# Layer B's residual read and added in the background, and sums of squares placed later on TensorE

## The chip, the cores and the metric

The kernel runs on one core of one Trainium2 chip. The metric is the time of one execution in microseconds of the device, a median over runs. A core has five engines that run side by side, each through its own queue, in program order: TensorE (PE in the profile) multiplies matrices, VectorE (DVE) and GpSimd (POOL) do elementwise work, ScalarE (ACT) does copies and functions, and SyncE (SP) issues the DMA transfers between the chip's memory (DRAM) and the on-chip memories. Matmul results arrive in PSUM, eight banks of 128 x 512 fp32, and everything else lies in SBUF.

## The reference

The reference is a decoder with two layers on 512 tokens and 16 learned meta tokens, width 2048. Layer A is a gated linear recurrence, layer B an attention with a forget gate. In its last part, which the change touches most, it computes

```python
h = h + fox_mix(h, ...)      # layer B: 16 heads, then  return (o * jax.nn.silu(z)) @ w_out
return h[:, N_META:]         # the meta tokens are dropped
```

Here `o * silu(z)` is a 512 x 2048 matrix, `w_out` is 2048 x 2048, and `h` is the residual, the output of layer A. Inside both layers vectors are normalised by `rms_norm(x, g) = x * rsqrt(mean(x*x) + eps) * g`, in layer B each head's q. The `mean(x*x)` are the sums of squares of the title.

## The kernel before, in words

**Precision.** Every fp32 matrix is split into a high part (a copy to the fp32r type on ACT) and a low part (the difference, on DVE), and a product of two matrices is three matmuls: high by high, high by low, low by high. For weights these are the tiles `w_raw` (as read), `w_hi` and `w_lo`; for the gated attention output they are `sh` and `sl`.

**The output projection of layer B** (lines 1861 to 1987) runs over four column blocks of 512 output columns, n = 0 to 3. Each block uses four PSUM tiles `pts`, one per 128 tokens, and adds products over 16 row groups k of 128 rows. Block 0 is plain: for each k four `o_step`s of three matmuls of 512 columns, 192 in all. Blocks 1 to 3 (`wide`, line 1887) save multiplications with a Strassen-like scheme over eight of the row groups: first four plain k as a lead (48 matmuls of 512 columns), then products 1, 6, 7, 5 into PSUM tiles `pp` of their own, then products 2, 4, 3 added into `pts` (7 x 24 matmuls of 256 columns), then the last four plain k (48 of 512 columns). Products 6, 7, 5, 3 use sums of row halves (`so`, formed once by `pair_sums` on POOL, `sums_o`), and products 6, 7, 5, 4 use sums of weight blocks (`w_sum`, made on DVE). Products 1, 6, 7, 5 make up the blocks `v1`, `v6`, `v7`, which POOL adds into the residual tile `hres`. The last step of a block is `ot = pts + hres` on DVE for each of four token groups, and a transfer of `ot` to DRAM. The two PSUM pools `psj` and `psj2` of four banks swap after each block, so that `pp` of a block takes over the banks of `pts` of the block before.

**The residual** lies in DRAM in a blocked form, `h1y`. `residual(n)` (line 1864) reads it by 16 transfers into `hraw` (one buffer) and rearranges it by four ACT copies into `hres` (two buffers). Block 0 does this after its last matmul in the program, a wide block at its very beginning, before its lead.

**Weights.** `Weights` (from line 218) keeps a list of units in the order of use. Raw weights are read through eight `w_raw` buffers, up to seven reads ahead of the unit in use (`dma_ahead=7`); a buffer is free again when the last unit that uses it has been split. Units are split up to a few ahead. `W.step()` (line 429) does as much of this as fits.

**What sets the order.** The whole program is written out by one Python program that keeps a planner's clock of every engine (`Clock`, line 39), and the order in which it emits instructions is the order in each engine's queue, SP's too. After every few matmuls `tick()` (line 719) calls `W.step()` and then goes once through the list `bg` of background tasks, which are generators. `do(f, ...)` (line 630) holds a task back until the planner's clock says that the instruction could start at most 900 ns (`LEAD`) after the time that PE has reached; a matmul in the background is held back until its inputs are written 1000 ns (`MARGIN`) before PE would come to it. `spin()` (line 727) advances the planner's PE clock by 150 ns without a matmul and calls `tick()`. So the planner decides on an order; on the chip each engine waits only for its own operands.

**Sums of squares.** Per token they are summed by a transpose and a reduction on DVE into `part`, and then by a small matmul of `part` with the constant `group` on PE (`token_sums`, line 664, for layer A, K and the stream; in `att_q`, line 1672, for the q of layer B, eight matmuls of 4 columns). The wait loops ahead of them, lines 670 and 1693, use the 1000 ns margin. In `att_q` the result leads to the factor `ry` (`qy` in the profile) that scales the scores `s` into logits `lg`.

Of the kernel before, what the change touches and what calls it, by code (L numbers as in the profile page):

```python
# [7 lines left out]
F32 = mybir.dt.float32  # L8
F32R = mybir.dt.float32r
AF = mybir.ActivationFunctionType  # L10
ALU = mybir.AluOpType
# [3 lines left out]
P = 128  # L15
D = 2048
KT = D // P
NH = 16
NM = 16
S = 512  # L20
# [8 lines left out]
NB3 = 1  # L29
# [458 lines left out]
def trunk(  # L488
# [5 lines left out]
    clock = Clock()  # L494
# [4 lines left out]
    def opened(stack, name, **kw):  # L499
        return Pool(stack.enter_context(tc.tile_pool(name=name, bufs=1, reuse_waits="tile", **kw)), name, clock)  # L500
# [61 lines left out]
    st_r = ExitStack()  # L562
# [16 lines left out]
    group = cp.tile([P, P], F32, name="group")  # L579
# [48 lines left out]
    act = se.activation  # L628

    def do(f, *args, **kw):  # L630

        while not f.fits(args, kw):
            yield
        f(*args, **kw)
# [29 lines left out]
    def token_sums(sq, t, w, psum, drop):  # L664

        nb = -(-w // 32)
        yield from fold(t, sq, w)
        part = cp.tile([P, 17], F32, name="part", tag="part", bufs=2)[:, :nb]
        yield from do(ve.tensor_reduce, part, folded(t[:, :32 * nb]), axis=mybir.AxisListType.X, op=ALU.add)
        while not te.matmul.fits((), {"lhsT": group, "rhs": part}):  # L670
            yield
        pt = yield from psum()
        te.matmul(pt[:, :nb], lhsT=group, rhs=part, start=True, stop=True)
        ss = cp.tile([P, 17], F32, name="ss", tag="ss", bufs=2)[:, :nb]
        yield from do(ve.tensor_copy, ss, pt[:, :nb])
        drop(pt)
        return ss
# [23 lines left out]
    bg = []  # L701
# [11 lines left out]
    def add(out, a, b):  # L713
        ve.tensor_tensor(out, a, b, op=ALU.add)
# [12 lines left out]
    def spin():  # L727

        clock.free["PE"] += 150
        tick()  # L730
# [285 lines left out]
    def blocks_in(t, d, nb):  # L1016

        for c in range(4):
            yield from do(sy.dma_start,
                t[c * 32:(c + 1) * 32],  # L1020
                d.rearrange("(g q) (c x) -> q g c x", q=32, c=4)[:, :, c, :])

    def blocks_now(t, d, nb):
        for c in range(4):
            sy.dma_start(
                t[c * 32:(c + 1) * 32],
                d.rearrange("(g q) (c x) -> q g c x", q=32, c=4)[:, :, c, :])

# [275 lines left out]
    for h in range(NH):  # L1304
        hd = {"h": h}
        if h == 0:
# [7 lines left out]
            raw = []  # L1314
# [111 lines left out]
    for n in range(KT):  # L1426
# [12 lines left out]
        g = h1_steps(n, pt, xr)  # L1439
# [232 lines left out]
    def att_q(h, uq):  # L1672
        a = A[h] = {"fin": set()}
        while sdone[0] < h:
            yield
        bg.append(att_load(h))
        sq = tb.tile([P, S], F32, name="nsq", tag="nsq")
        yield from do(act, sq, uq, AF.Square)
        g = gqs[:, h:h + 1]
        qh = tb.tile([P, 3 * P], F32R, name="qh", tag="qh")  # L1680
        ql = tb.tile([P, 3 * P], F32R, name="ql", tag="ql")
        yield from do(act, qh, uq[:, P:], AF.Identity, scale=g)
        yield from do(ve.scalar_tensor_tensor, ql, uq[:, P:], g, qh.bitcast(F32), ALU.mult, ALU.subtract)
        qg = tb.tile([P, P], F32, name="qg", tag="qg")
        yield from do(ge.tensor_scalar, qg, uq[:, :P], g, None, ALU.mult)
        free_u("buq")
        a.update(qg=qg, q=(qh, ql))
        ss, y, t1, t2 = (tb.tile([P, 4], F32, name=n, tag=n, bufs=2) for n in ("qs", "qy", "qt1", "qt2"))
        t = tb.tile([P, S], F32, name="nss", tag="nss")
        yield from fold(t, sq, S)  # L1690
        part = cp.tile([P, 17], F32, name="part", tag="part", bufs=2)[:, :16]
        yield from do(ve.tensor_reduce, part, folded(t), axis=mybir.AxisListType.X, op=ALU.add)
        while not te.matmul.fits((), {"lhsT": group, "rhs": part}):
            yield
        pt = psj.tile([P, 512], F32, name="pj1", tag="pj", bufs=pjb[0])
        for j in range(4):
            te.matmul(pt[32 * j:32 * (j + 1), :4], lhsT=group[:, :32],
                      rhs=part.rearrange("p (i j) -> p j i", j=4)[:, j], start=True, stop=True)
        yield from do(ve.tensor_copy, ss, pt[:, :4])
        yield from rstd_steps(y, ss, P, t1, t2)  # L1700
        a["ry"] = y
# [159 lines left out]
    movo = LazySplit(S)  # L1861
    outv = out[0].rearrange("(b p) n -> p b n", p=P)

    def residual(n):

        raw = ob.tile([P, 4, S], F32, name="hraw", tag="hraw")
        hr = ob.tile([P, 4, S], F32, name="hres", tag="hres", bufs=2)
        for j in range(4):
            blocks_now(raw[:, j, :].rearrange("p (g x) -> p g x", g=4), h1y[4 * n + j], 4)
        for b in range(4):  # L1870
            act(hr[:, b, :].rearrange("p (j f) -> p j f", f=32),
                raw.rearrange("p j (g b f) -> p (j g) b f", g=4, f=32)[:, :, b, :], AF.Copy)
        return hr

    def finish(n, b, pt, hr):
        ot = ob.tile([P, S], F32, name="ot", tag="ot", bufs=4)
        ve.tensor_tensor(ot, pt, hr[:, b, :], op=ALU.add)
        sy.dma_start(outv[:, b, n * 512:(n + 1) * 512], ot)

    def o_step(pt, w, k, b, first, last):  # L1880
        wh, wl, _ = w
# [5 lines left out]
    def wide(n):  # L1887

        us = nt_unit[("bo", n)]
        comb = residual(n)  # L1890

        def cb(r, c):
            return comb[:, 2 * r:2 * r + 2, c * 256:(c + 1) * 256]

        def x(e, r):
            return lambda i, q: [t[:, (2 * r + q) * P:(2 * r + q + 1) * P] for t in movo[2 * i + e]]
# [16 lines left out]
        def add(out, a, b):  # L1913
            ve.tensor_tensor(out, a, b, op=ALU.add)
# [8 lines left out]
        for v, xs in ((1, x(0, 0)), (6, s(0, 1)), (7, s(1, 0)), (5, s(0, 0))):  # L1923
            while v == 6 and sums_o in bg:
                spin()
            pp[v] = psj2.tile([P, 512], F32, name="pj1", tag="pj", bufs=4)
            product(v, xs, [v4(pp[v])[:, q] for q in range(2)])
            if v != 5:
                vv[v] = ob.tile([P, 512], F32, name=f"v{v}", tag=f"v{v}")
            if v == 1:  # L1930
                act(vv[1], pp[1], AF.Copy)
                ge.tensor_tensor(cb(0, 0), cb(0, 0), v4(vv[1]), op=ALU.add)
            elif v == 6:
                add(vv[6], pp[6], vv[1])
            elif v == 7:
                add(vv[7], pp[7], vv[6])
                ge.tensor_tensor(cb(1, 0), cb(1, 0), v4(vv[7]), op=ALU.add)
            else:
                add(vv[6], pp[5], vv[6])
                add(vv[7], pp[5], vv[7])  # L1940
                ge.tensor_tensor(cb(0, 1), cb(0, 1), v4(vv[6]), op=ALU.add)
                ge.tensor_tensor(cb(1, 1), cb(1, 1), v4(vv[7]), op=ALU.add)
        for v, xs, r, c in ((2, x(1, 0), 0, 0), (4, x(1, 1), 1, 0), (3, s(1, 1), 0, 1)):
            product(v, xs, [pts[2 * r + q][:, c * 256:(c + 1) * 256] for q in range(2)], False)
        tail = 3 if n == ng - 1 else 0
        for k in range(2 * KB + LEAD, KT - tail):
            w = W.get(us["k", k])
            for b in range(4):
                o_step(pts[b], w, k, b, False, k == KT - 1)
        wt = [W.get(us["k", k]) for k in range(KT - tail, KT)]  # L1950
        for b in range(4):
            ot = ob.tile([P, S], F32, name="ot", tag="ot", bufs=4)
            for k, w in enumerate(wt, KT - tail):
                o_step(pts[b], w, k, b, False, k == KT - 1)
            add(ot, pts[b], comb[:, b, :])
            sy.dma_start(outv[:, b, n * 512:(n + 1) * 512], ot)

    ng = D // 512
# [1 line left out]
    for n in range(ng):  # L1960
        if n >= NB3:
            wide(n)
            psj, psj2 = psj2, psj
            continue
        pts = [psj.tile([P, 512], F32, name="pj1", tag="pj", bufs=4) for _ in range(4)]
        units_n = nt_unit[("bo", n)]
        for k in range(KT):
            if n == 0 and k == 10:
                drain()
                pss.close()  # L1970
                st_l.close()
                so = opened(st_l, "b_sums")
                psj2 = opened(pss, "psj_o", space=PSUM)
                sums_o = pair_sums(movo, lambda j: so.tile([P, S], F32R, name=f"so{j}", tag=f"so{j}"),
                                   lambda j: so.tile([P, S], F32, name=f"sm{j}", tag=f"sm{j}"), S_o, KB, S, ge)
                W.more(lambda nm, w, dt: so.tile([P, w], dt, name=nm, tag=nm), 4, len(W.units))
                bg.append(sums_o)
            w = W.get(units_n[k])
            for b in range(4):
                o_step(pts[b], w, k, b, k == 0, k == KT - 1)  # L1980
        if n == 0:
            st_r.close()
            ob = opened(st_r, "b_out", side="right")
            hr = residual(n)
        psj, psj2 = psj2, psj
        for b in range(4):
            finish(n, b, pts[b], hr)
    drain()
    pss.close()
    st_r.close()  # L1990
# [32 lines left out]
```

## Time and profile before

| | |
|---|---|
| median of 3 runs | 2060.08 us (2059.97 to 2061.24) |
| the profiled execution | 2068.14 us, of which the span from first to last instruction is 2066.4 us |
| mean granted TensorE clock | 0.986 of full speed |
| PE, busy | 2004.8 us (97%), 14676 matmuls |
| DVE, busy | 1522.8 us (74%) |
| ACT, busy | 948.0 us (46%) |
| POOL, busy | 445.4 us (22%) |
| issues of weight reads for the last stage | 64 of 256 KB, 3.7 us to landing in the median |

Busy time is the time in which an engine executes instructions; issuing DMAs does not count as such. Almost every line of the profile bears L194, because one helper emits all instructions, so they are told apart by the names of the tiles: `pj` are the PSUM tiles of the projections, and numbers of buffers are left out, so `w_sum` stands for all weight sums and `v` for `v1`, `v6` and `v7`. Times in a timeline count from the first instruction. A number in brackets at the end of a row is the idle time of the engine just ahead of it, and what it waited for.

### The profile page before, as it was taken

How to read it: one execution, taken by the hardware profiler on the slowest of the kernel's cores; microseconds unless marked ns; L12 is line 12 of the kernel's file. 1: busy time of each engine (PE TensorE's matmuls, PEld its weight loads, DVE VectorE, ACT ScalarE, POOL GpSimd, SP SyncE). 2: the span in 40 equal slices, each digit the busy share in tenths (PEclk: the TensorE clock that was granted, in tenths of full speed). 3: DMA queues.
4: the chain of work that ended last, by engine and by line, in shares of the span. 5: the costliest groups of instructions: out<-in, count | busy, mean ns of one | idle time of the engine just before them, and what ended most of it. 6: DMA issues, size and time to landing. Idle time of an engine off the chain costs nothing.

```text
span 2066.4 us, 39517 instructions
## 1 busy us (share of the span) xinstructions
PE 2004.8 (97%) x14676; PEld 1871.9 (91%) x14676; DVE 1522.8 (74%) x3025; ACT 948.0 (46%) x1756; POOL 445.4 (22%) x527
## 2 busy tenths in 40 slices
PE   8999999999999999999999999999999999999798
PEld 7999999999999999899999999998777777877687
DVE  6878888888888886544498777866777777777554
ACT  6655454545454454423333333334555555554322
POOL 2121111111112121111100000002444433455111
PEclk9999999999999999999999999999999999999899
DMA  8333333333334335345534444465555565553342
GB/s 265 99 111 107 107 110 113 107 106 107 106 107 118 107 110 178 90 154 161 162 86 135 125 134 111 117 187 154 154 149 153 159 165 141 148 144 112 123 136 94
DMA packets 454337, 271.21 MB, mean 131 GB/s; under 512 B 77936, under 2 KB 420448, under 8 KB 454128
## 3 DMA queue, kind: packets, MB, share of 16 engines
q1 hardware_dynamic: 452576, 264.16, 44.8%
q0 software_dynamic: 1536, 4.52, 0.6%
q8 instruction: 115, 1.88, 0.4%
q14 instruction: 78, 0.64, 0.1%
q10 hardware_dynamic: 32, 0.01, 0.0%
HBM read 220.30 MB, written 48.28 MB: 130 GB/s over the span
## 4 chain that ended last, share of the span: by engine, by line
PE 77%; DMA 6%; DVE 5%; SPq 4%; issue 3%; ACT 2%; POOL 2%; ACTq 0%; DVEq 0%; POOLq 0%
PE pj L194 71%; SPq L194 4%; DMA py<-pd 3%; PE o L194 2%; PE tr L194 2%; PE pat L194 1%; DVE w_lo L194 1%; POOL sm L194 1%; DVE lg L194 1%; DMA w_raw<-in_b_w_in_dram 1%; POOL D L194 1%; ACT w_hi L194 1%; PE s L194 1%; DVE sm L194 1%; DMA w_raw<-in_b_w_out_dram 1%
## 5 line engine op out<-in xcount | busy, mean ns | idle before, releaser
L194 PE MATMUL pj<-sh,w_hi 128*128 128x264 f32 (+1 forms) x2604 | 755.2, 314 | 4.3 <-ACT sh L194 3.3
L194 PE MATMUL pj<-sl,w_hi 128*128 128x264 f32 (+1 forms) x2604 | 737.6, 307 | 1.1 <-DVE sl L194 1.1
L194 PE MATMUL pj<-sh,w_lo 128*128 128x264 f32 (+1 forms) x2604 | 736.2, 307 | 1.2 <-DVE w_lo L194 1.2
L194 DVE TENSOR_TENSOR w_lo<-w_raw,w_hi 128x512 fp32r<-128x512 f32 (+1 forms) x585 | 431.8, 751 | 86.7 <-ACT w_hi L194 85.7
L194 PEld LDWEIGHTS pj<-sh,w_hi 128*128 128x128 f32 x2604 | 467.6, 190 | 25.6 <-ACT sh L194 3.9
L194 PEld LDWEIGHTS pj<-sh,w_lo 128*128 128x128 f32 x2604 | 466.4, 189 | 24.5 <-DVE w_lo L194 2.2
L194 PEld LDWEIGHTS pj<-sl,w_hi 128*128 128x128 f32 x2604 | 468.3, 190 | 20.0 <-DVE sl L194 1.8
L194 ACT ACTIVATE w_hi<-w_raw 128x512 fp32r<-128x512 f32 (+1 forms) x585 | 353.3, 621 | 176.3 <-PE pj L194 137.3
L194 PE MATMUL pj<-sm,w_hi 128*128 128x264 f32 x896 | 172.9, 289 | 0.0
L194 PEld LDWEIGHTS pj<-sm,w_hi 128*128 128x128 f32 x896 | 138.5, 188 | 1.7
L194 ACT ACTIVATE w_hi<-w_sum 128x512 fp32r<-128x512 f32 x102 | 63.2, 625 | 162.9 <-POOL w_sum L194 88.7
L194 PE MATMUL pj<-sm,w_lo 128*128 128x264 f32 x448 | 127.4, 284 | 0.0
L194 POOL TENSOR_TENSOR w_sum<-w_sum,w_raw 128x512 f32<-128x512 f32 x28 | 43.6, 1556 | 374.4 <-DVE w_sum L194 195.4
L194 ACT ACT_TABLE_LOAD x87 | 111.6, 1283 | 11.6 <-DVE uq L194 3.8
L194 PE MATMUL pj<-kh,w_hi 128*128 128x264 f32 x460 | 115.6, 285 | 0.0
L194 PE MATMUL pj<-kl,w_hi 128*128 128x264 f32 x460 | 115.1, 284 | 0.0
L194 PE MATMUL pj<-kh,w_lo 128*128 128x264 f32 x460 | 114.7, 283 | 0.0
L194 DVE TENSOR_TENSOR w_lo<-w_sum,w_hi 128x512 fp32r<-128x512 f32 x102 | 80.8, 793 | 15.8 <-ACT w_hi L194 15.0
L194 PE MATMUL pj<-w_hi,sh 128*128 128x512 f32 (+1 forms) x232 | 84.0, 362 | 4.8 <-ACT sh L194 4.8
L194 PE MATMUL pj<-kh,sh 128*128 128x264 f32 x324 | 87.2, 285 | 0.0
L194 PE MATMUL pj<-kl,sh 128*128 128x264 f32 x324 | 86.9, 284 | 0.0
L194 PE MATMUL pj<-kh,sl 128*128 128x264 f32 x324 | 86.8, 284 | 0.0
(387 smaller groups left out, 3610.4 us busy)
## 6 DMA issues: line engine op xcount, KB each, us to landing
w_raw<-in_a_w_in_dram SPq DMA_DIRECT2D x256, 256.0 KB, 3.4
w_raw<-in_kv_w_dram SPq DMA_DIRECT2D x128, 256.0 KB, 4.1
w_raw<-in_b_w_in_dram SPq DMA_DIRECT2D x128, 256.0 KB, 3.2
w_raw<-in_a_w_out_dram SPq DMA_DIRECT2D x64, 256.0 KB, 4.0
w_raw<-in_b_w_out_dram SPq DMA_DIRECT2D x64, 256.0 KB, 3.7
xr<-xT SPq DMA_DIRECT2D x16, 264.0 KB, 4.4
h1T<-h SPq DMA_DIRECT2D x16, 264.0 KB, 2.0
kT<-kn SPq DMA_DIRECT2D x16, 264.0 KB, 2.1
```

What stands on the lines that cost most here:

```text
L194: ins = f(*args, **kw)
```

## The change

Five things change.

1. The wait loops ahead of the matmuls of the sums of squares ask for 2000 ns instead of 1000 between the end of the reduction and the matmul.
2. `residual(n)` becomes a background task: its 16 reads and four copies are emitted one by one when they fit. Block 0's is read by the task `finish`, which is put on the list when block 0's matmuls are emitted; the same task goes on to read residual 1. The residuals 2 and 3 are put on the list in the block before, after product 5.
3. `finish` also holds the four adds and transfers of block 0. Before block 1 emits product 1, it spins until `finish` has emitted them.
4. The adds of `v1`, `v6`, `v7` into `hres` become background tasks (`add_block`), which wait until the residual is there. The add of product 5 into `v7` moves into the task of that block, behind the POOL add that reads `v7`. A wide block spins until its tasks are through before it emits its final adds (in the last block: before its last three k).
5. The pool of the output buffers is opened two k earlier, inside block 0.

```diff
-        while not te.matmul.fits((), {"lhsT": group, "rhs": part}):
+        while clock.ready("PE", [], [part], 2 * clock.MARGIN) > clock.free["PE"]:
             yield
 ...
+    hres = {}
+
     def residual(n):
 
         raw = ob.tile([P, 4, S], F32, name="hraw", tag="hraw")
+        for j in range(4):
+            yield from blocks_in(raw[:, j, :].rearrange("p (g x) -> p g x", g=4), h1y[4 * n + j], 4)
         hr = ob.tile([P, 4, S], F32, name="hres", tag="hres", bufs=2)
-        for j in range(4):
-            blocks_now(raw[:, j, :].rearrange("p (g x) -> p g x", g=4), h1y[4 * n + j], 4)
         for b in range(4):
-            act(hr[:, b, :].rearrange("p (j f) -> p j f", f=32),
-                raw.rearrange("p j (g b f) -> p (j g) b f", g=4, f=32)[:, :, b, :], AF.Copy)
-        return hr
-
-    def finish(n, b, pt, hr):
-        ot = ob.tile([P, S], F32, name="ot", tag="ot", bufs=4)
-        ve.tensor_tensor(ot, pt, hr[:, b, :], op=ALU.add)
-        sy.dma_start(outv[:, b, n * 512:(n + 1) * 512], ot)
+            yield from do(act, hr[:, b, :].rearrange("p (j f) -> p j f", f=32),
+                          raw.rearrange("p j (g b f) -> p (j g) b f", g=4, f=32)[:, :, b, :], AF.Copy)
+        hres[n] = hr
+
+    def block_of(n, r, c):
+        return hres[n][:, 2 * r:2 * r + 2, c * 256:(c + 1) * 256]
+
+    adding = []
+
+    def add_block(n, r, c, v, more=None):
+
+        adding.append((n, r, c))
+        if more is not None:
+            while (n, r, 0) in adding:
+                yield
+            yield from do(ve.tensor_tensor, v, more, v, op=ALU.add)
+        while n not in hres:
+            yield
+        t = block_of(n, r, c)
+        yield from do(ge.tensor_tensor, t, t, v.rearrange("p (q n) -> p q n", q=2), op=ALU.add)
+        adding.remove((n, r, c))
+
+    def finish(n, pts):
+
+        adding.append(n)
+        yield from residual(n)
+        for b in range(4):
+            ot = ob.tile([P, S], F32, name="ot", tag="ot", bufs=4)
+            yield from do(ve.tensor_tensor, ot, pts[b], hres[n][:, b, :], op=ALU.add)
+            yield from do(sy.dma_start, outv[:, b, n * 512:(n + 1) * 512], ot)
+        adding.remove(n)
+        yield from residual(n + 1)
 ...
     def wide(n):
-        comb = residual(n)
 ...
         for v, xs in ((1, x(0, 0)), (6, s(0, 1)), (7, s(1, 0)), (5, s(0, 0))):
             while v == 6 and sums_o in bg:
                 spin()
+            while n == NB3 and NB3 - 1 in adding:
+                spin()
 ...
             if v == 1:
                 act(vv[1], pp[1], AF.Copy)
-                ge.tensor_tensor(cb(0, 0), cb(0, 0), v4(vv[1]), op=ALU.add)
+                bg.append(add_block(n, 0, 0, vv[1]))
 ...
             else:
                 add(vv[6], pp[5], vv[6])
-                add(vv[7], pp[5], vv[7])
-                ge.tensor_tensor(cb(0, 1), cb(0, 1), v4(vv[6]), op=ALU.add)
-                ge.tensor_tensor(cb(1, 1), cb(1, 1), v4(vv[7]), op=ALU.add)
+                bg.append(add_block(n, 0, 1, vv[6]))
+                bg.append(add_block(n, 1, 1, vv[7], pp[5]))
+                if n < ng - 1 and n >= NB3:
+                    bg.append(residual(n + 1))
 ...
+        while adding:
+            spin()
         for b in range(4):
 ...
-            add(ot, pts[b], comb[:, b, :])
+            add(ot, pts[b], hres[n][:, b, :])
 ...
+            if n == 0 and k == KT - 2:
+                movo.upto(KT)
+                st_r.close()
+                ob = opened(st_r, "b_out", side="right")
 ...
-        if n == 0:
-            st_r.close()
-            ob = opened(st_r, "b_out", side="right")
-            hr = residual(n)
         psj, psj2 = psj2, psj
-        for b in range(4):
-            finish(n, b, pts[b], hr)
+        bg.append(finish(n, pts))
```

## Rows read from the trace of the kernel before

**Rows 1.** The page, part 1: busy us, share of the span, instructions of each engine.
```profile
PE 2004.8 (97%) x14676; PEld 1871.9 (91%) x14676; DVE 1522.8 (74%) x3025; ACT 948.0 (46%) x1756; POOL 445.4 (22%) x527
```

**Rows 2.** Waits of TensorE, whole span: us in total, times, longest us.
```profile
PE pj L194 <- ACT w_hi L194: 17.1, 4, 12.0
PE pj L194 <- DVE part L194: 9.4, 7, 2.6
...
PE s L194 <- DVE lg L194: 3.1, 2, 2.9
```

**Rows 3.** Timeline of TensorE, blocks 0 and 1: start, us, operation [idle before <-releaser].
```profile
1909.53 0.40 PE L194 MATMUL pj<-w_hi,sh 128*128 128x512 f32 x1
...
1916.25 0.39 PE L194 MATMUL pj<-w_hi,sl 128*128 128x512 f32 x1
1916.48 0.28 PE L194 MATMUL pj<-w_hi,sh 128*128 128x256 f32 x1
...
1919.20 0.28 PE L194 MATMUL pj<-w_hi,sl 128*128 128x256 f32 x1
1931.48 0.58 PE L194 MATMUL pj<-w_hi,so 128*128 128x256 f32 x1 [11.99 <-ACT w_hi L194]
```

**Rows 4.** Timeline of TensorE, blocks 2 and 3.
```profile
1975.90 0.28 PE L194 MATMUL pj<-w_hi,sh 128*128 128x256 f32 x1
...
1980.76 0.38 PE L194 MATMUL pj<-w_hi,so 128*128 128x256 f32 x1 [1.86 <-ACT w_hi L194]
...
2024.20 0.28 PE L194 MATMUL pj<-w_hi,sh 128*128 128x256 f32 x1
...
2029.93 0.58 PE L194 MATMUL pj<-w_hi,so 128*128 128x256 f32 x1 [2.72 <-ACT w_hi L194]
...
2061.39 0.40 PE L194 MATMUL pj<-w_hi,sl 128*128 128x512 f32 x1
```

**Rows 5.** Stretches: length, busy us of the engines, PEclk, DMA share, GB/s.
```profile
1900.00:1910.00 10.00, 9.80 (x42) 8.01 (x43) 9.13 (x8) 2.39 (x5) 9.76 (x9) 1.00 0.00 0
...
1930.00:1940.00 10.00, 7.68 (x31) 6.80 (x32) 8.10 (x13) 4.60 (x8) 0.21 (x1) 0.50 0.25 81
...
1980.00:1990.00 10.00, 8.40 (x43) 7.91 (x44) 8.73 (x13) 5.09 (x9) 1.76 (x1) 0.66 0.27 88
...
2030.00:2040.00 10.00, 9.36 (x55) 8.77 (x56) 9.05 (x14) 4.58 (x9) 1.76 (x1) 0.70 0.29 99
```

**Rows 6.** Timeline of SP's queue, the issue of DMAs, first two seams.
```profile
1890.66 7.58 SPq L194 DMA_DIRECT2D hraw<-h1y  x16
...
1913.29 3.60 SPq L194 DMA_DIRECT2D out_dram<-ot  x4
1917.06 7.54 SPq L194 DMA_DIRECT2D hraw<-h1y  x16
1924.65 2.48 SPq L194 DMA_DIRECT2D w_raw<-in_b_w_out_dram  x5
...
1966.11 8.53 SPq L194 DMA_DIRECT2D hraw<-h1y  x16
1974.73 14.58 SPq L194 DMA_DIRECT2D w_raw<-in_b_w_out_dram  x9
```

**Rows 7.** Timelines of ACT, DVE and POOL at the first two seams.
```profile
1911.84 2.18 ACT L194 ACTIVATE hres<-hraw 128x512 f32<-128x512 f32 x4
...
1911.97 0.69 DVE L194 TENSOR_TENSOR so<-sm,so 128x512 fp32r<-128x512 f32 x1 [0.15 <-ACT so L194]
1912.58 2.48 DVE L194 TENSOR_TENSOR ot<-pj,hres 128x512 f32<-128x512 f32 x4
1928.40 0.69 DVE L194 TENSOR_TENSOR w_sum<-w_raw 128x512 f32<-128x512 f32 x1 [13.35 <-DMA w_raw<-in_b_w_out_dram]
...
1981.27 1.76 POOL L194 TENSOR_TENSOR hres<-hres,v 128x512 f32<-128x512 f32 x1 [32.05 <-ACT v L194]
```

**Rows 8.** DMA issues: operation, count, KB each, median us from issue to landing.
```profile
hraw<-h1y SPq DMA_DIRECT2D x64, 64.0 KB, 2.1
```

More of the change, by code (lines that the diff above doesn't have):

```diff
@@ L1019, in blocks_in @@
             yield from do(sy.dma_start,
[L1020 to L1025, printed above, removed]
                 t[c * 32:(c + 1) * 32],
@@ L1692, in att_q @@
         yield from do(ve.tensor_reduce, part, folded(t), axis=mybir.AxisListType.X, op=ALU.add)
-        while not te.matmul.fits((), {"lhsT": group, "rhs": part}):
+        while clock.ready("PE", [], [part], 2 * clock.MARGIN) > clock.free["PE"]:
             yield
@@ L1889, in wide @@
         us = nt_unit[("bo", n)]
-        comb = residual(n)
-        def cb(r, c):
-            return comb[:, 2 * r:2 * r + 2, c * 256:(c + 1) * 256]
         def x(e, r):
@@ L1936, in wide @@
                 add(vv[7], pp[7], vv[6])
-                ge.tensor_tensor(cb(1, 0), cb(1, 0), v4(vv[7]), op=ALU.add)
+                bg.append(add_block(n, 1, 0, vv[7]))
             else:
                 add(vv[6], pp[5], vv[6])
-                add(vv[7], pp[5], vv[7])
-                ge.tensor_tensor(cb(0, 1), cb(0, 1), v4(vv[6]), op=ALU.add)
-                ge.tensor_tensor(cb(1, 1), cb(1, 1), v4(vv[7]), op=ALU.add)
+                bg.append(add_block(n, 0, 1, vv[6]))
+                bg.append(add_block(n, 1, 1, vv[7], pp[5]))
+                if n < ng - 1 and n >= NB3:
+                    bg.append(residual(n + 1))
         for v, xs, r, c in ((2, x(1, 0), 0, 0), (4, x(1, 1), 1, 0), (3, s(1, 1), 0, 1)):
```

## The prediction

> **What bounds the kernel now.** I read the busy times of the page first, then the waits of TensorE, then the timeline around the longest of them, and last the queues of the engines that TensorE waited for. TensorE is busy 97% of the span [rows 1], so only time in which it stands still, or runs at the lower clock, can be won. Its list of waits is short. One line leads it: 17.1 us in four waits for the high half of a weight (ACT w_hi), the longest 12.0 us; the second is 9.4 us in seven waits for `part`, the partial sums of squares [rows 2]. Every other line is below those.
>
> The four waits on w_hi lie in the last stage, the output projection of layer B, which the change rewrites. To see what that stage loses I price its matmuls where they run undisturbed: 30 matmuls of 512 columns start from 1909.53 to 1916.25, so 6.72/29 = 0.232 us each; the 24 of 256 columns of product 1 start from 1916.48 to 1919.20, so 0.118 us each [rows 3]. A wide block has 96 of the first and 168 of the second: 22.3 + 19.8 = 42.1 us. Product 1 of the three wide blocks starts at 1916.48, 1975.90 and 2024.20 [rows 3, 4]: the first period is 59.4 us, the second 48.3, so 17.3 and 6.2 us too long. From 2024.20 to the last matmul at 2061.39 it is 37.2 us, against 168 x 0.118 + 48 x 0.232 = 31.0: 6.2 too long. **Lost in the stage: 29.7 us.** In each period the loss sits between products 1 and 6: 11.99 us of waiting at 1931.48, 1.86 at 1980.76, 2.72 at 2029.93 [rows 3, 4], and behind each gap a stretch granted 0.50, 0.66 and 0.70 of the full clock [rows 5], so partly or wholly the 1.2 GHz level.
>
> Why is w_hi late? Product 6 needs a sum of two weight blocks (w_sum). Its DVE instruction starts at 1928.40, after standing idle for 13.35 us until a weight had landed [rows 7]. That weight was read late because of SP's queue, which is strictly in program order: it issued the reads of residual 0 from 1890.66, then held four output transfers that waited for the last adds (1913.29), then sixteen reads of residual 1 (7.54 us from 1917.06), and only at 1924.65 the next weight reads. At the next seam the weights start at 1974.73, behind residual reads that hold the queue for 8.53 us [rows 6].
>
> **The change part by part.** Apart from order, nothing is added: per block still 16 residual reads on SP, 4 copies on ACT, 4 adds on POOL (none for block 0), 4 adds on DVE, 4 output transfers.
>
> *Reads of residuals 2 and 3.* They move from the head of a wide block into the second half of the block before it. On SP they leave some 8.5 us per seam [rows 6] to the weight reads, which then follow the four output transfers directly: the reads that started at 1974.73 start near 1966.1. Product 1 ends near 1978.8, and the wait was 1.86 us, so they are early by some 6 us. SP has room: a block issues 16 weight reads, 16 residual reads and 4 outputs, 36 x 0.47 = 17 us of 42. The reads wait for the single raw buffer, which the ACT copies of the residual before have left long ago; were they late, the weight reads would be queued behind them, and TensorE behind those. The four copies on ACT (2.18 us, [rows 7]) move past weight splits that are made several units ahead. These two seams lose 12.4 us; I leave 2 of it, for the adds that now run beside the weight work: gain 10.4, bounds 4 and 12.4.
>
> *Residual 0 and the end of block 0.* Reads, copies, adds and outputs of block 0 become a background task that starts when the block's matmuls are issued, and product 1 of the next block may not be issued before it is through, since it takes over block 0's PSUM buffers. This is a new wait on TensorE: behind it stands everything. The planner gives the task 11.1 us of lead matmuls (48 x 0.232). The 16 reads take 7.5 us to issue, one lands in 2.1 us [rows 8], the copies take 2.2, the first add 0.7: 12.5 us if it started only with the lead. But SP has been idle since 1898, so on the chip the reads go out early, between the weight reads that step in at each k. The first add can start as before, near 1912.6, when the last split of the pair sums (the `so` at 1911.97) is done [rows 7]; product 1 wants its buffer at 1916.48. The wait of 12.0 us goes. What is late next is DVE: from 1912.6 to the start of the fourth product it has 4 adds of block 0, 6 sums, 6 low halves and 2 adds to do, 18 x 0.62 = 11.2 us (0.62 from the four adds in 2.48 us, [rows 7]), in 12.4 us. That packs only if their order is right, so of 17.3 us I leave 4 (a short wait and some slow clock): gain 13.3. Bounds: 0, if the seam stalls as long on its new wait, and 17.3.
>
> A rule speaks against these two parts. The trace shows that sixteen issues hold SP for 7.54 us while one such read lands in 2.1 us [rows 6, 8]. The Trainium skill, "DMA: Bandwidth & Descriptors", section "Issuing engines are not separate DMA queues", says that the time a sequencer needs to initiate a DMA is usually small beside the DMA itself. By that rule the place of the reads in the queue would matter little and the sum would shrink to its last term; by the row it is the place that costs. Small strided reads are where I side with the row.
>
> *Adds of the blocks (POOL) and the last product.* The four adds per wide block are issued once the residual is there. The DVE add of product 5 into v7 waits, as before, until POOL has read v7; low halves are queued behind it. The final adds wait for POOL too. Cost taken 0: POOL does nothing else there, and the last add of a block needs TensorE's last matmul anyway. If POOL were late at the very end, one of its adds, 1.76 us [rows 7], would show: bound 2.
>
> *Sums of squares later on TensorE.* The planner now keeps 2000 instead of 1000 ns between the reduction on DVE and the matmul that uses it, so about four more 512-column matmuls go ahead of it. In layer B seven groups waited, 9.4 us, the longest 2.6 us [rows 2]. Each gets shorter by up to 1 us: at most 7.0; some are shorter than 1 us, so I take 6. Lower bound 0, if TensorE then waits for the logits instead; upper bound 9.4. In the first layer and for K, TensorE shows no wait on `part`: taken 0, bound 3 lost where a later result reaches the end of a stage.
>
> Sum: 10.4 + 13.3 + 6 = 29.7, rounded to 30 us. The profiled execution took 2068.1 us, 8.1 above the median of 2060.1 (its span is 2066.4); 2068.1 - 30 = 2038 under the profiler, and the same off the median is **2030 us**.
>
> **Rivals.** (1) *The first seam stays.* The background task is drawn out by its sixteen waits for the planner's clock, or DVE works off weight sums ahead of block 0's adds, and product 1 stalls where product 6 did. For it: the 12.5 us chain against 11.1 us of lead. Against: the reads may run ahead on SP. Then 17.3 us stay and 10.4 + 6 = 16 go: 2044. (2) *Bytes, not places.* Each residual is 1 MB in small pieces; if weights land late because both share the DMA engines, moving helps nothing, and only the 6 us of `part` are won: 2054. This is the skill's rule above turned into a time. Against: the queue was held, not the engines, and no bytes moved from 1900 to 1910, just before the wait [rows 5]. (3) *Slower.* The later sums of squares delay the factor that scales the logits, so the three PSUM tiles of the scores come free later and TensorE waits for `lg` in every head, as it did once for 2.9 us [rows 2]. At 2.9 us in 16 heads that is 46 us against 30 won: 2076. It decides from 30/16 = 1.9 us per head. Against: the line holds 3.1 us in all, so 14 of the 16 heads have slack on this path. (4) *No net change.* Order in the first layers shifts with the new margin and loses what the end wins: 2060.
>
> **How the numbers follow.** Chances: forecast 0.64, (1) 0.19, (2) 0.05, (3) 0.07, (4) 0.05. Faster by over 0.2% (4.1 us, about what a measurement can tell): 0.64 + 0.19 + 0.05 = 0.88; within: 0.05; slower: 0.07. Range: with all gains at their upper bounds, 12.4 + 17.3 + 9.4 = 39, it is 2021, so the low end is 2020; the high end, 2050, takes in rival (1) with the lower bound of the other seams (4 instead of 10.4: 2048). That leaves out (2), (3) and (4), 0.17, and a little of the tails.
>
> **What would show it.** The waits of TensorE on w_hi near 1931, 1980 and 2030 gone or under 2 us, no stretch below 0.9 of the clock after 1900; w_raw reads directly behind the output transfers on SP; periods of the wide blocks near 43 to 46 us; the line on `part` below 4 us. A wait of product 1 on the adds of block 0 means rival (1); longer waits on `lg` mean rival (3); weights that still land late, though issued early, mean rival (2).

## The result, and the profile after

| | before | after |
|---|---|---|
| median | 2060.66 us (2059.97 to 2066.78, 4 runs) | 2038.34 us (2034.93 to 2041.51, 4 runs) |
| ratio of the two | | 0.9885, 95% interval 0.9869 to 0.9900 |
| the profiled execution | 2068.14 us, span 2066.4 | 2041.51 us, span 2039.8 |
| mean granted TensorE clock | 0.986 | 0.993 |

The change makes the kernel 22.3 us faster by the medians, 23.7 by the ratio (21 to 27 by its interval) and 26.6 us by the two profiled executions. The forecast was 2030 us.

TensorE is again the engine that is nearly always busy; it does the same 14676 matmuls in 7.6 us less [rows 1]. Page, part 1, after:

```profile
PE 1997.2 (98%) x14676; PEld 1863.2 (91%) x14676; DVE 1519.3 (74%) x3025; ACT 950.3 (47%) x1757; POOL 439.5 (22%) x527
```

The waits of TensorE over the whole span after (us in total, times, longest):

```profile
PE o L194 <- ACT PTh L194: 5.7, 6, 2.1
PE pj L194 <- ACT sh L194: 4.6, 4, 1.6
PE s L194 <- DVE lg L194: 4.6, 2, 2.8
...
PE pj L194 <- DVE part L194: 3.2, 4, 1.5
PE pj L194 <- ACT w_hi L194: 2.8, 1, 2.8
```

Against [rows 2], the line on w_hi has gone from 17.1 us in four waits to one of 2.8, and the one on `part` from 9.4 to 3.2. But a line that was lower down before, the matmuls of `o` (a head's output) that wait for `PTh` (the high part of the transposed scores), now leads.

Where in time the gain lies is read from the timeline of TensorE after. A seam is the passage from one column block to the next, and a period runs from one product 1 to the next. The rows show product 1 of the three wide blocks, the one wait left, and the last matmul (start, us, operation, idle before).

```profile
1914.23 0.28 PE L194 MATMUL pj<-w_hi,sh 128*128 128x256 f32 x1
...
1920.70 0.58 PE L194 MATMUL pj<-w_hi,so 128*128 128x256 f32 x1 [2.75 <-ACT w_hi L194]
...
1962.32 0.28 PE L194 MATMUL pj<-w_hi,sh 128*128 128x256 f32 x1
...
2004.46 0.28 PE L194 MATMUL pj<-w_hi,sh 128*128 128x256 f32 x1
...
2035.22 0.40 PE L194 MATMUL pj<-w_hi,sl 128*128 128x512 f32 x1
```

With [rows 3, 4] this splits the 26.17 us by which the last matmul starts earlier (all in us):

| stretch | before | after | gain | forecast |
|---|---|---|---|---|
| up to product 1 of block 1 | 1916.48 | 1914.23 | 2.25 | 6 |
| first period | 59.42 | 48.09 | 11.33 | 13.3 |
| second period | 48.30 | 42.14 | 6.16 | 10.4 for the two |
| from 2024.20 / 2004.46 to the last matmul | 37.19 | 30.76 | 6.43 | |

The second and third period are now as long as their matmuls take undisturbed (42.1 and 31.0); the first still has 6 us too much. The stretches of the clock agree (length, busy us of the engines, PEclk, DMA share, GB/s): the stretch with the wait of 2.75 us is granted 0.66. The two at the later seams, which had 0.66 and 0.70 [rows 5], get the full clock.

```profile
1920.00:1930.00 10.00, 9.15 (x53) 8.86 (x54) 8.99 (x15) 5.65 (x10) 0.00 (x0) 0.66 0.75 221
1965.00:1975.00 10.00, 10.00 (x86) 10.00 (x85) 8.68 (x14) 5.48 (x10) 2.04 (x2) 1.00 0.48 157
...
2010.00:2020.00 10.00, 10.00 (x86) 10.00 (x86) 10.00 (x14) 4.84 (x8) 4.24 (x3) 1.00 0.16 56
```

What is left at the first seam shows in SP's queue after, against [rows 6] (issue of DMAs: start, us, transfer, count):

```profile
1889.37 7.58 SPq L194 DMA_DIRECT2D hraw<-h1y  x16
1897.05 0.39 SPq L194 DMA_DIRECT2D w_raw<-in_b_w_out_dram  x1
1912.87 1.82 SPq L194 DMA_DIRECT2D out_dram<-ot  x2
1914.78 0.39 SPq L194 DMA_DIRECT2D w_raw<-in_b_w_out_dram  x1
1915.27 0.92 SPq L194 DMA_DIRECT2D out_dram<-ot  x2
...
1951.32 2.13 SPq L194 DMA_DIRECT2D out_dram<-ot  x4
1953.54 21.62 SPq L194 DMA_DIRECT2D w_raw<-in_b_w_out_dram  x12
```

The reads of residual 0 still go out early and in one piece. At 1897.05 one weight read follows, and then SP stands for 15 us in front of two output transfers of block 0; the next weight read leaves only at 1914.78. At the second seam the weights follow the outputs directly, as forecast. Why the outputs were late, and what hung on the read behind them, ACT and DVE show after, against [rows 7] (the same columns):

```profile
1909.55 0.63 ACT L194 ACTIVATE so<-sm 128x512 fp32r<-128x512 f32 x1 [0.76 <-POOL sm L194]
1910.09 2.18 ACT L194 ACTIVATE hres<-hraw 128x512 f32<-128x512 f32 x4
...
1912.16 0.68 DVE L194 TENSOR_TENSOR ot<-pj,hres 128x512 f32<-128x512 f32 x1
...
1918.49 0.69 DVE L194 TENSOR_TENSOR w_sum<-w_raw 128x512 f32<-128x512 f32 x1 [2.98 <-DMA w_raw<-in_b_w_out_dram]
```

The copies into `hres` stand behind the last split of the pair sums on ACT, which waits for POOL; the first add of block 0 (`ot`) follows at 1912.16. DVE then idles 2.98 us, until 1918.49, for the weight that was read at 1914.78. That sum feeds product 6, which waits 2.75 us.

### The profile page after: what moved, and what is told of

It is laid out like the page before. It is cut to its first block, busy times and chain, and to the rows that moved or that the text cites. A ratio compares the mean times of both kernels' runs of the same rounds, so it can differ in the third digit from the quotient of the medians.

```text
span 2039.8 us, 39552 instructions
## 1 busy us (share of the span) xinstructions
PE 1997.2 (98%) x14676; PEld 1863.2 (91%) x14676; DVE 1519.3 (74%) x3025; ACT 950.3 (47%) x1757; POOL 439.5 (22%) x527
## 4 chain that ended last, share of the span: by engine, by line
PE 80%; DMA 6%; DVE 5%; issue 3%; ACT 2%; SPq 2%; POOL 2%; ACTq 0%; DVEq 0%; POOLq 0%
PE pj L194 74%; DMA py<-pd 2%; PE o L194 2%; PE tr L194 2%; SPq L194 2%; PE pat L194 2%; DVE w_lo L194 1%; DVE lg L194 1%; POOL sm L194 1%; DMA w_raw<-in_b_w_in_dram 1%; DMA pd<-py 1%; DMA vtk<-vd 1%; DVE sm L194 1%; DVE py L194 1%; DMA Fb<-Fd 1%
## 5 line engine op out<-in xcount | busy, mean ns | idle before, releaser
L194 DVE TENSOR_TENSOR w_lo<-w_raw,w_hi 128x512 fp32r<-128x512 f32 (+1 forms) x585 | 441.6, 766 | 95.1 <-ACT w_hi L194 93.7
L194 PE MATMUL pj<-w_hi,sl 128*128 128x512 f32 (+1 forms) x232 | 84.1, 363 | 2.3 <-DVE sl L194 2.3
```

What stands on the lines that cost most here:

```text
L194: ins = f(*args, **kw)
```

## The experiments

All ratios are to the kernel before, measured beside it on the same chip; its medians there were 2060.66 to 2063.11 us. 0.001 is 2.06 us. "o margin" and the other edits are explained below.

| kernel | median us | ratio (95%) | product 1 | three periods |
|---|---|---|---|---|
| changed kernel | 2038.34 | 0.9885 (0.9869 to 0.9900) | 1914.2 | 48.1, 42.1, 30.8 |
| e1 later sums of squares alone | 2059.97 | 0.9990 (0.9980 to 1.0000) | 1912.0 | 54.7, 49.2, 37.6 |
| e2 residual alone | 2037.86 | 0.9874 (0.9859 to 0.9889) | 1913.7 | 45.9, 42.1, 30.8 |
| e3 outputs behind weights | 2034.30 | 0.9860 (0.9846 to 0.9875) | 1911.6 | 42.7, 43.6, 30.8 |
| e4 residual read twice | 2044.20 | 0.9909 (0.9893 to 0.9924) | 1913.9 | 46.8, 46.5, 33.6 |
| e5 residuals at the head | 2050.66 | 0.9940 (0.9921 to 0.9960) | 1912.1 | 48.4, 48.6, 36.9 |
| e6 e3 + o margin | 2028.91 | 0.9836 (0.9820 to 0.9852) | 1906.9 | 42.1, 45.2, 30.8 |
| e7 e3 + gates first | 2036.80 | 0.9874 (0.9859 to 0.9890) | 1909.4 | 42.7, 47.7, 30.8 |
| e8 e7, old margin of `part` | 2038.41 | 0.9884 (0.9867 to 0.9901) | 1915.0 | 42.7, 47.2, 30.8 |
| e9 e6, old margin of `part` | 2027.60 | 0.9835 (0.9817 to 0.9854) | 1900.9 | 42.1, 46.7, 30.8 |
| e10 e6, 3000 ns for `part` | 2029.03 | 0.9841 (0.9820 to 0.9862) | 1904.4 | 42.8, 42.2, 30.8 |
| e11 e6 again | 2028.11 | 0.9832 (0.9815 to 0.9850) | 1903.4 | 42.1, 45.2, 30.8 |

The last two columns are of the profiled execution, from the timeline of TensorE: the start of product 1 of block 1, and the two periods and the stretch from the last product 1 to the last matmul, in us. e6 and e11 are one program, and its product 1 starts 3.5 us apart in two executions: differences of that size in this column alone mean nothing.

**e1: the sums of squares alone.** The kernel before, with only the two wait loops changed.

```diff
-        while not te.matmul.fits((), {"lhsT": group, "rhs": part}):
+        while clock.ready("PE", [], [part], 2 * clock.MARGIN) > clock.free["PE"]:
```

> The kernel before with only the two wait loops of the sums of squares changed (2000 instead of 1000 ns of margin); the residual as before. Theory A (the gain is the residual's alone; the wait on part only changes its name): no change against the kernel before, within 2 us, with the waits of TensorE on part down from 9.4 us to about 3 and those on PTh, lg and w_lo up by about as much. Theory B (the forecast's term): 6 us faster than before, 2054, with no other wait longer.

The time is the same within 0.2%. In layer B (1410 to 1848 us) TensorE's waits before were those on `part` (9.4 us, all of its line in [rows 2]), on `lg` (3.1) and small ones, 16.8 us in sum; `PTh` had

```profile
PE o L194 <- ACT PTh L194: 2.0, 2, 1.3
```

In e1:

```profile
PE o L194 <- ACT PTh L194: 6.2, 6, 1.7
PE pj L194 <- DVE part L194: 3.6, 4, 1.8
PE s L194 <- DVE lg L194: 2.8, 2, 1.6
PE pj L194 <- DVE w_lo L194: 1.8, 1, 1.8
```

With three smaller ones the sum is 17.0. The wait on `part` fell by as much as forecast, and others rose by as much, `PTh` (by 4.2) and `w_lo` (by 1.3) above all. The changed kernel shows the same: 5.7 on `PTh`, 4.6 on `lg`, 3.2 on `part`, 2.3 on `w_lo`, 0.9 on `buq`, 16.7 in sum.

**e2: the residual alone.** The changed kernel with the two old loops. Residual n + 1 here starts only when residual n has been copied, which holds in e4 and e6 to e11 too.

```diff
     def residual(n):
+        while n and n - 1 not in hres:
+            yield
```

> The changed kernel with the old 1000 ns loops, so the residual part alone (one guard more: a residual's reads start only when the copies of the one before are issued). Theory A: as fast as the changed kernel, within 2 us, about 22 us faster than before. Theory B: 6 us slower than the changed kernel, about 2044; the waits on part are back at about 9 us.

Its ratio is 0.0011 below the changed kernel's, inside both intervals, and its first period is 2.2 us shorter, which is as much. With e1 this puts the gain in the last stage; what the margin adds is too small for these intervals.

**e3: block 0's outputs behind the weights.** If the weight read that stood behind the outputs is the cause of the 6 us left, it must go when the outputs are emitted behind the first ten weight reads of the next block.

```diff
-            yield from do(sy.dma_start, outv[:, b, n * 512:(n + 1) * 512], ot)
+            ots.append(ot)
         adding.remove(n)
+        while W.nd < first_src[n + 1] + 10:
+            yield
+        for b in range(4):
+            yield from do(sy.dma_start, outv[:, b, n * 512:(n + 1) * 512], ots[b])
```

> The changed kernel, but block 0's four output transfers are issued only after the reads of all weights that product 6 of block 1 needs. It tests what holds the 6 us that are left at the first seam (product 1 to product 1 takes 48.1 us there and 42.1 at the next). Theory SP (a weight read stands behind output transfers that wait for the last adds): the wait of 2.75 us ahead of product 6 goes and with it the slow clock behind it; the period comes down to 42 to 44 us, 4 to 6 us faster than the changed kernel, about 2033. Theory DVE (the adds, sums and splits of that stretch don't pack): the wait stays above 1.5 us with another releaser than a DMA behind the sum, gain under 2 us.

It went. In SP's queue of e3 two weight reads stand ahead of the outputs where one stood, TensorE no longer waits ahead of product 6, and the first period falls from 48.1 to 42.7. 0.0025 of the ratio goes with it, 4 us by the medians and 5 by the ratios. The second period is 1.5 us longer, so the stage gains 3.9 of the 5.4.

```profile
1886.79 7.60 SPq L194 DMA_DIRECT2D hraw<-h1y  x16
1894.49 0.90 SPq L194 DMA_DIRECT2D w_raw<-in_b_w_out_dram  x2
1910.28 4.33 SPq L194 DMA_DIRECT2D out_dram<-ot  x4
```

**e4: every residual read twice.** To price the bytes: each of the 64 reads is issued a second time, into `hres`, which the copies overwrite.

```diff
-            yield from blocks_in(raw[:, j, :].rearrange("p (g x) -> p g x", g=4), h1y[4 * n + j], 4)
+            for t in (raw, hr):
+                yield from blocks_in(t[:, j, :].rearrange("p (g x) -> p g x", g=4), h1y[4 * n + j], 4)
```

> The changed kernel with every residual read issued twice (the second time into the tile that the copies overwrite), so 16 more transfers of 64 KB and 7.5 us more of SP's queue per block. Theory place (what counts is whether a weight read stands behind something that waits): at most 3 us slower than the changed kernel, all of it at the first seam, periods 2 and 3 stay at 42 us. Theory bytes or issue time (the reads cost the same wherever they stand): 7 us or more per seam are back, some 20 us slower, about 2058.

0.0024 over the changed kernel and 0.0035 over e2, so 5 to 7 us for 64 issues and 4 MB more: neither theory's number. Nor is it at the first seam, where the place theory had put it, since the periods that grew are the second and third. In the first period the wait ahead of product 6 is gone and another has come, at the start of block 2:

```profile
1943.44 1.29 POOL L194 TENSOR_TENSOR hres<-hres,v 128x512 f32<-128x512 f32 x1 [34.30 <-ACT hres L194]
1947.49 4.17 POOL L194 TENSOR_TENSOR hres<-hres,v 128x512 f32<-128x512 f32 x3 [2.76 <-ACT hres L194]
...
1950.05 0.72 PE L194 MATMUL pj<-w_hi,sh 128*128 128x512 f32 x1 [2.91 <-DVE v L194]
```

Residual 1 is complete later, so POOL adds `v7` late, so the DVE add of product 5 into `v7` is late, and with it the PSUM bank that the next block's lead needs: 2.91 us. That is the cost which the forecast took as 0 for the adds on POOL; it appears once the residual is late. It lies ahead of product 1 of block 2, so it isn't what made the later periods longer. What did shows on DVE and TensorE at the second seam:

```profile
1951.67 0.69 DVE L194 TENSOR_TENSOR w_lo<-w_raw,w_hi 128x512 fp32r<-128x512 f32 x1 [1.77 <-ACT w_hi L194]
1952.28 2.48 DVE L194 TENSOR_TENSOR ot<-pj,hres 128x512 f32<-128x512 f32 x4
1961.88 0.69 DVE L194 TENSOR_TENSOR w_sum<-w_raw 128x512 f32<-128x512 f32 x1 [7.13 <-DMA w_raw<-in_b_w_out_dram]
...
1966.27 0.39 PE L194 MATMUL pj<-w_lo,so 128*128 128x256 f32 x1 [1.78 <-DVE w_lo L194]
```

The final adds of block 1 stand behind low halves that wait for late weights, and start 8.4 us before product 1 of block 2 (11.7 in the changed kernel); at the third seam it is 7.4. Behind the adds come the outputs and the next weight reads, and product 6 waits again, for 2.2 us in sum at the second seam and 2.1 at the third. The weight reads themselves land in 3.9 us in the median in both kernels, so they are late because they are issued late. What the bytes cost apart from the 64 issues isn't shown.

**e5: residuals 2 and 3 at the head of their blocks.** The same reads and copies as in the changed kernel, in the place that they had before.

```diff
+        if n > NB3:
+            residual_now(n)
 ...
-                if n < ng - 1 and n >= NB3:
-                    bg.append(residual(n + 1))
```

> The changed kernel with one part undone: residuals 2 and 3 are read and copied at the head of their block, in the foreground, as before; the first seam and the sums of squares stay changed. Theory place: the weight reads stand behind sixteen residual reads again, the periods 2 and 3 grow from 42.1 and 30.8 us to 48 and 37, and the kernel is 10 to 13 us slower than the changed one, about 2050. Theory slack (the two seams owe their gain to something else in the change, such as the later adds): less than 5 us slower.

The two later periods are back at 48.6 and 36.9 (before 48.3 and 37.2), and 0.0055 of the ratio, 11 us, is lost with them. SP, DVE and TensorE of e5:

```profile
1948.29 2.35 SPq L194 DMA_DIRECT2D out_dram<-ot  x4
1950.70 8.97 SPq L194 DMA_DIRECT2D hraw<-h1y  x16
1959.77 26.32 SPq L194 DMA_DIRECT2D w_raw<-in_b_w_out_dram  x16
...
1963.72 0.69 DVE L194 TENSOR_TENSOR w_sum<-w_raw 128x512 f32<-128x512 f32 x1 [13.43 <-DMA w_raw<-in_b_w_out_dram]
...
1965.94 0.51 PE L194 MATMUL pj<-w_hi,so 128*128 128x256 f32 x1 [2.44 <-ACT w_hi L194]
...
2016.59 0.39 PE L194 MATMUL pj<-w_lo,so 128*128 128x256 f32 x1 [2.59 <-DVE w_lo L194]
```

The same bytes cost 11 us by their place, and doubling them costs 5 to 7: what counts is the time for which 16 issues hold the queue, 8.97 us here, ahead of reads that the next products need. The copies on ACT went back to the head as well, but the sum for product 6 waits on DVE for the weight (13.43 us), not for ACT.

**e6: a later start for the `o` matmuls.** If a wait in layer B is only handed on, from `part` to `PTh`, it should go when the receiver gets the 2000 ns as well. The loop ahead of the `o` matmuls in e3, changed like those in e1:

```diff
-        while not all(te.matmul.fits((), {"lhsT": v, "rhs": w}) for v, w in (
-                (a["v"][0], PTh), (a["v"][1], PTl), (a["v3"], PT3), (a["vc"], Z[h % 2]))):
+        while clock.ready("PE", [], [*a["v"], PTh, PTl, a["v3"], PT3, a["vc"], Z[h % 2]], 2 * clock.MARGIN) > clock.free["PE"]:
```

> The kernel with block 0's outputs behind the weights, and also 2000 instead of 1000 ns of margin ahead of the matmuls that use the softmax result (PTh) in layer B. The longer margin for the sums of squares had moved 4 us of waiting from part to PTh. Theory moved (each margin hands the wait to the next link of a head's chain): the wait on PTh falls from 7.2 to under 3 us, but others rise, and the time changes by under 2 us. Theory sum (the waits can be taken away one after the other): 4 us faster than the kernel with the outputs behind the weights, about 0.984 of the kernel before.

0.0024 below e3, 5 us, and again in e11 (0.0028). The intervals of e3 and e6 overlap a little; all four kernels with this margin, e6 and e9 to e11, lie below e3's interval, and e7 and e8, which have all of e6's edits but this margin and one line more, don't. The three periods are no shorter (118.1 us in sum, 117.1 in e3), so the gain lies ahead of product 1. Layer B of e6 has waits of 15.7 us in sum against 17.8 in e3 (and 13.7 in e11); the line on `PTh`, 7.2 us in e3, is down to 0.3, but those on `part`, `sl` and `w_lo` have grown:

```profile
PE pj L194 <- DVE part L194: 6.7, 6, 2.3
PE pj L194 <- DVE sl L194: 3.8, 1, 3.8
PE pj L194 <- DVE w_lo L194: 3.3, 4, 1.3
...
PE o L194 <- ACT PTh L194: 0.3, 1, 0.3
```

**e7 and e8: the gates first.** In e7, which is e3 with one more line (and the wait for the residual before, as in e6), the gated outputs `sh`, `sl` are all made before the pair sums, to take the waits on them out of block 0. e8 is e7 with the old loops.

```diff
                 st_l.close()
+                movo.upto(KT)
                 so = opened(st_l, "b_sums")
```

> The kernel with block 0's outputs behind the weights, and with the splits of the last gate tiles (sh, sl) issued before the pair sums of block 0 instead of among them. In it TensorE waits 2.6 us in block 0 for sh and sl, which stand on ACT and DVE behind pair sums that wait for POOL. Theory queue: these waits go, 2 to 3 us faster than that kernel, about 0.9845 of before. Theory late sums: the pair sums end later and product 6 of block 1 waits for them instead; no gain or a loss.

> The kernel of the run with all gates first, but with the old 1000 ns ahead of the sums of squares. It repeats the question of the margin in the fastest setting. Theory A (the wait only moves): within 2 us of that run, either side. Theory B (the forecast's term): 6 us slower.

e7 brought nothing: the waits on `sh` and `sl` went, product 1 started at 1909.4, and the second period gave it back (47.7). DVE of e7 shows the final adds of block 1 behind two low halves that wait for ACT, and ACT made copies of residual 2 at that time:

```profile
1942.97 1.15 ACT L194 ACTIVATE hres<-hraw 128x512 f32<-128x512 f32 x2 [1.81 <-DMA w_raw<-in_b_w_out_dram]
...
1944.68 0.69 DVE L194 TENSOR_TENSOR w_lo<-w_raw,w_hi 128x512 fp32r<-128x512 f32 x1 [2.79 <-ACT w_hi L194]
1946.24 0.69 DVE L194 TENSOR_TENSOR w_lo<-w_raw,w_hi 128x512 fp32r<-128x512 f32 x1 [0.87 <-ACT w_hi L194]
1946.85 2.48 DVE L194 TENSOR_TENSOR ot<-pj,hres 128x512 f32<-128x512 f32 x4
1955.48 0.69 DVE L194 TENSOR_TENSOR w_sum<-w_raw 128x512 f32<-128x512 f32 x1 [6.15 <-DMA w_raw<-in_b_w_out_dram]
```

Late adds make late output transfers, and the weight reads stand behind those. The adds start 5.2 us before product 1 of block 2, against 11.7 in the changed kernel, where DVE then waits just as long for a weight (6.17 us) and TensorE not at all; here TensorE waits 2.62 us. It is the first seam's fault at the second seam. e8 equals e7 within 0.0010.

**e9 to e11: is the margin of `part` worth something once `o` has its own?** e9 takes it back to 1000 ns in e6, e10 raises it to 3000 ns in `att_q`, e11 is e6 again.

```diff
-        while clock.ready("PE", [], [part], 2 * clock.MARGIN) > clock.free["PE"]:
+        while clock.ready("PE", [], [part], 3 * clock.MARGIN) > clock.free["PE"]:
```

> The kernel of e6_later_o_matmuls with the changed kernel's 2000 ns taken back to 1000 ns for the adds of the sums of squares; the same margin for the o matmuls stays. Theory sum (in layer B the waits of PE add up; a wait that is taken away is paid back by the next one in the chain, and only where all links have slack does time go): with the o matmuls no longer waiting early, the wait on part comes back at about 9 us in layer B and stays there; 4 to 6 us slower than e6_later_o_matmuls, so about 2034. Theory moved (the wait only changes its row whatever the other margins are): within 2 us of e6_later_o_matmuls, about 2029, with a sum of PE's waits in layer B that is unchanged at some 15 us.

> The kernel of e6_later_o_matmuls with 3000 ns in place of 2000 for the sums of squares in att_q only. Theory sum: the wait on part that e6_later_o_matmuls still shows in layer B (6.7 us in 6) falls to under 3, and 3 to 4 us go: about 2025. Theory moved: within 2 us of e6_later_o_matmuls, with the wait on other rows (sl, w_lo, PTh).

> e6_later_o_matmuls again, beside the two: 2029, within 2 us of its first time, by either theory; its layer B waits again 15 to 16 us in sum.

All three are one time within 0.0009 of the ratio, so the theory behind e6's expectation, that the waits add up and each margin gives its share, falls for `part`. In e10 its wait in layer B is as good as gone, and a wait for the first gated outputs of block 0 takes its place:

```profile
PE pj L194 <- ACT sh L194: 5.6, 1, 5.6
PE pj L194 <- DVE w_lo L194: 2.2, 3, 1.7
...
PE pj L194 <- DVE part L194: 0.7, 1, 0.7
```

In e9 the line on `part` is at 7.9 us in 7 waits, all waits of layer B come to 11.1 (15.7 and 13.7 in e6 and e11), and the kernel is no slower. The pairs that differ in this margin are now e1 and before, the changed kernel and e2, e7 and e8, e6 (or e11) and e9: -0.0010, +0.0011, -0.0010, +0.0001 (or -0.0003) of the ratio, with no sign in common. Why the margin of `o` gives 5 us and that of `part` nothing isn't shown.

## Why the prediction was right, and where it was not

The sign, the size class and the place were right, and the time lies in the range; the point was 8 us too low.

*The two later seams* were forecast at 10.4 and gained 12.6, all that was lost there: the weight reads follow the outputs directly, and no wait is left. e5 shows that the move of the reads does this, by taking the move back. The place of the reads mattered because 16 issues in a row hold SP for 7.58 us after, too, and in e5 for 8.97, while one such read lands in 2.1 us [rows 8]. The rule weighed in the prediction (the Trainium skill, "DMA: Bandwidth & Descriptors", "Issuing engines are not separate DMA queues") says that the time to initiate a DMA is usually small beside the DMA itself. For one read that is 0.47 us (7.58/16) against 2.1, so about a quarter; for sixteen in a row it is the larger part, and the prediction was right to side with the row. Rival (2), bytes, is refuted by e5; twice the issues and bytes, in e4, cost 5 to 7 us.

*The first seam* was forecast at 13.3 and gained 11.3. The mechanism held, the reads of residual 0 ran ahead, and product 1 did not stall on the new wait, so rival (1) did not come. But the prediction named DVE's packing as what would be late next, and that was wrong: DVE was idle for 2.98 us. What is late is one weight read behind block 0's output transfers in SP's queue. The prediction took SP's order at this seam as solved by moving the reads, and did not ask what the outputs themselves hold up. e3 shows it: 5.4 us of this period, 4 to 5 of the time. So three of the signs named for the end fail at this seam alone: no stretch below 0.9 of the clock (0.66), a period of 43 to 46 us (48.1), and a wait under 2 us (2.75).

*The two sizes cancel*, and that is luck: 23.9 us for the last stage against 23.7. Against the stage of e1, whose execution was near the median, it is 20.4.

*The sums of squares* are the step that failed: forecast 6, bounds 0 and 9.4, measured 2 in e1 (0 to 4), and nothing that the intervals tell from zero in three other pairs. The wait on `part` did fall, 9.4 to 3.2, as worked out; what failed is to take the shorter wait for time won. The lower bound said that TensorE might wait for the logits instead. In the changed kernel it waits for `lg` 1.5 us longer, for `PTh` 3.7 and for `w_lo` 1.8; in e1 `lg` holds no more than before (2.8). Rival (3), 2.9 us in each of 16 heads, did not come: `lg` holds 4.6 us in two waits. In the first layer and for K the trace shows no change, as taken: the first wait of layer B's projections, on `buq`, ends at 1414.96, before at 1415.10.

*The base.* By the profiled executions the gain is 26.6 us of the 30, and the rest of the miss lies in subtracting it from the median. The profiled execution of before took 8.1 us more than the median, and the losses were read from it. e1 has the same last stage and ran at 2059.9 under the profiler: its three periods are 26.2 us too long, not 29.7, its first 54.7 and not 59.4. So a part of the 29.7 belongs to that execution; with 22.3 us between the medians, some 4 us. How much of this varies from run to run was not measured. These 4 us and the 4 that the sums of squares did not bring make up the miss of 8.

*The range.* Its high end rests on a slip: rival (1) with the lower bound of the other seams is 2060 less 4 and 6, so 2050 and not 2048, and 2050 leaves nothing over. The measured time did not come near it.

The changed kernel leaves about 10 us on the table: e6, e9 and e11, all with the outputs behind the weights and the later `o` matmuls, run at 0.9832 to 0.9836, against 0.9885, and are the fastest kernels here (e10, with the same two edits, 0.9841).

## What to carry to other kernels

Read a queue that issues in order as a list of what each entry waits for: transfers that wait for results (outputs) belong behind reads that wait for nothing and are needed soon, and long runs of small reads belong where the queue is idle. A wait that gets shorter in the profile is time won only if the next instruction that it gates is not waiting for something else; change that one alone and time it before adding it into a sum. And price losses from an execution near the median, or from two, when the profiled one stands well above it.

## What was not expected of the hardware

A seam costs more than its wait. Behind the single wait of 2.75 us in the changed kernel the four microseconds from 1922 to 1926 were granted 0.50 of the clock, the 1.2 GHz level, and the first period came out 6.0 us too long. In e6 two waits of 1.54 and 0.80 us made the second period 3.1 us too long, with the full clock behind them. In e9 two of 1.75 and 0.80 us at the same place were followed by 0.50 from 1950 to 1952, and it was 4.6 too long. So waits of nearly one length can be followed by either level; what decides isn't shown. And reads that nobody needed, 4 MB in 64 KB pieces, cost 5 to 7 us in all, where the theory that charges for bytes or issue time had put some 20.
